# A weight chunk's low part by an accumulating transfer, in a two-layer decoder trunk

## The chip, the cores and the metric

The kernel runs on one core of a Trainium2 chip. The metric is the device time of one execution in microseconds (us); lower is better. Profiles show one execution, and their spans run from its first to its last instruction.

## What is computed

The trunk has two layers over 256 tokens of width 1024, batch 1, all in float32. Cut to what matters here:

```python
for l in range(DEPTH):                        # 2 layers
    h = rmsnorm(x, norm_g[l])
    q, k, v, ga, iq, ik, iw, xr, gr, ma, mb = split(h @ w_in[l])
    attn = dsa_attention(rope(q), rope(k), v, rope(iq), rope(ik), iw)   # top 64 keys by an indexer
    y_a = (attn * silu(ga)) @ w_out_attn[l]
    hr = rg_lru(conv4(xr), w_rg[l], w_ig[l], ...)                       # gates, then a scan over tokens
    y_b = (hr * silu(gr)) @ w_out_rnn[l]
    x = x + (sigmoid(ma) * y_a + sigmoid(mb) * y_b) @ w_o[l]
return rmsnorm(x, final_g)
```

## The kernel before

**Products in three passes.** A float32 product is made from float32r parts: a matrix W is split into a high part wh (W rounded to float32r) and a low part wl = W - wh, the activations likewise, and TensorE adds wh·h_high, wl·h_high and wh·h_low in PSUM (`mm3`, lines 640 to 644). So each 128x128 block of weights takes three matmuls.

**The weight stream.** The host lays all weights out as 225 chunks of 512 KB, 128 partitions by 1024 columns, 8 blocks each, in the order in which TensorE is to use them (`weight_stream`, and the class `Stream` from line 528). A chunk is loaded from SP's queue into one of four buffers `raw` (line 519). `chunk` (line 552) makes the two parts: `copy(wh, raw)`, a copy that rounds, and `sub(wl, raw, wh)`, a subtraction on VectorE (line 486 in the helper `tt`). The copy runs on ScalarE (line 480), or on VectorE (line 482) where the planner finds that ScalarE would begin it over 500 ns later. `wh` and `wl` have six buffers each (`WBUF`). The first two chunks are split in halves into other tiles (`whh`, `whl`).

**The order within a layer** (`plan`, line 65): the unit `head` (32 blocks: the index key, the index weights and three of the index queries) takes four chunks; then come the index queries `iq` 3, 4 and 5, a chunk each (in layer 0 these are chunks 4, 5 and 6), the first unit of `ga`, and after it the other index queries, the recurrent inputs `xr` and `gr`, the gates, the merge gates `ma` and `mb` and the rest of `ga`. All this is called the early part here: 492 blocks, 61.5 chunks, in each layer. Then follow `q`, `k`, `v` and the attention, and last the output projections `yb`, `ya` and `wo`. In `head`, the rotation (`rotate`, line 773) makes `ikr` from the bank `pk` with the tables `ctab_i` and `stab_i` (sines on ScalarE, lines 687 and 688) scaled to `ci` and `si`; `iwt` is the last reader of the bank `pk`, and `ga` needs a bank of that pool. From `ikr` come `kh` and `kl`, which the indexer's `dots` need (line 871); ScalarE takes their positive part as `rl`, and VectorE sums `rl` into `wk`. GpSimd masks `wk` with `affine_select` (`causal`, line 891, instruction on line 895), four times per layer.

**What sets the order.** No order is written by hand: `Program.issue` (line 285) is a list planner. Each operation has an engine, a planned cost and, after it, a planned latency by engine (`LATENCY`, line 227). Due times are carried back from TensorE's position in the stream (`deadlines`, line 371), weight conversions 2000 ns earlier (`LEAD`). `choose` (line 394) takes, for each engine, the candidate that can start first, then the one due first, and a buffer of a ring must be free in the plan. At the end the instructions are written out sorted by planned start (line 367), each engine's in that order; on the chip semaphores hold each one until what it needs is done. The planner's engines are TensorE, ScalarE, VectorE, GpSimd and SP's transfers.

The conversion, lines 566 to 571:

```python
                wh = pg.tile(wp, "wh", [P, 1024], F32R, nm("wh"), WBUF)
                wl = pg.tile(wp, "wl", [P, 1024], F32R, nm("wl"), WBUF)
                copy(wh, raw)
                sub(wl, raw, wh.bitcast(F32))
                pg.shift = 0.0
                self.parts[c] = (wh, wl)
```

Of the kernel before, what the change touches and what calls it, by code (L numbers as in the profile page):

```python
# [11 lines left out]
F32 = mybir.dt.float32  # L12
F32R = mybir.dt.float32r
I32 = mybir.dt.int32
AF = mybir.ActivationFunctionType
OP = mybir.AluOpType
# [4 lines left out]
L = 2  # L21
# [43 lines left out]
def plan(l):  # L65

    u = [("head",)]
    iq = [("iq", i) for i in range(8)]
    light = []
    for n, i in (("ga", 0), ("mb", 0), ("ga", 1), ("mb", 1), ("ga", 2), ("ma", 0), ("ga", 3), ("ma", 1)):  # L70
        light += [(n, 2 * i), (n, 2 * i + 1)] if n == "ga" else [(n, i, c) for c in range(4)]
    u += iq[3:NRAW]
    for i in range(NRAW, 8):
        u += light[:NMIX] + [iq[i]]
        light = light[NMIX:]
    for j in range(KR):
        u += [("xr", j), ("gr", j)]
        u += light[:2 if j % 3 == 0 else 1]
        light = light[2 if j % 3 == 0 else 1:]
        if j >= DELAY:  # L80
            u.append(("gate", j - DELAY))
    for j in range(KR - DELAY, KR):
        u += light[:2]
        light = light[2:]
        u.append(("gate", j))
    u += light
    for pr in range(4):
        u += [("q", 2 * pr), ("q", 2 * pr + 1), ("k", 2 * pr), ("k", 2 * pr + 1)]
        if pr % 2 == 0:
            u += [("v", pr // 2, c) for c in range(4)]  # L90
        u.append(("attn", pr))
    u += [("yb", n) for n in range(2)]
    if l == L - 1:
        return u + [("xt", 0), ("ya", 0), ("xt", 1), ("ya", 1), ("wt", 0), ("wt", 1)]
    u += [("ya", n) for n in range(2)]
    return (u + [("wo", m, 0, 4) for m in range(6)] + [("wo", m, 4, 8) for m in range(6)]
            + [("wo", m, 0, 8) for m in range(6, 8)])


def gate_parts(j):  # L100


    f = foreign(j)
    if 2 * len(f) <= P:
        return [("stack", f)]
    return [("plain", f[:-STACK]), ("stack", f[-STACK:])]
# [13 lines left out]
def unit_blocks(u):  # L120

    n = u[0]
    if n == "head":
        return [b for k in range(KD)
                for b in [("in80", k, OFF["ik"])] + [("in", k, OFF["iq"] + i * P) for i in range(3)]]
    if n in ("attn", "xt"):
        return []
    if n in ("iq", "ga", "xr", "gr", "q", "k"):
        return [("in", k, OFF[n] + u[1] * P) for k in range(KD)]
    if n == "gate":  # L130
        out = []
        for w in ("rg", "ig"):
            out.append((w, u[1], u[1] * P))
            out += [(w, tuple(rows * (2 if kind == "stack" else 1)), u[1] * P) for kind, rows in gate_parts(u[1])]
        return out
    if n in ("v", "mb", "ma"):
        return [("in", 2 * u[2] + k, OFF[n] + u[1] * 512 + a * P) for k in range(2) for a in range(4)]
    if n == "yb":
        return [("or", k, u[1] * 512 + a * P) for k in range(KR) for a in range(4)]
    if n == "ya":  # L140
        return [("oa", k, u[1] * 512 + a * P) for k in range(KD) for a in range(4)]
    if n == "wt":
        return [("o", k, u[1] * 512 + a * P) for k in range(KD) for a in range(4)]
    return [("o", k, u[1] * P) for k in range(u[2], u[3])]
# [3 lines left out]
NCH = -(-NBLK // 8)  # L148


class H:


# [55 lines left out]
def real(a):  # L209
    return a.ap() if isinstance(a, V) else a  # L210
# [12 lines left out]
TABS[AF.Sqrt] = ("sqrt",)  # L223
TABS[AF.Sin] = ("sin",)
PSUM_TAGS = ("pp", "pq", "pt")
ENGINES = ("pe", "act", "dve", "pool", "dma")
LATENCY = {"pe": 190.0, "act": 140.0, "dve": 130.0, "pool": 200.0, "dma": 2000.0}
TO_PE = 230.0
SWITCH = 1283.0

# [1 line left out]
class Program:  # L232
# [52 lines left out]
    def issue(self):  # L285
# [13 lines left out]
        for o in ops:  # L299
            for h in o.uses:  # L300
                left[id(h)] = h.users
        free = {e: 0.0 for e in ENGINES}
        pending = {e: [] for e in ENGINES}

# [13 lines left out]
        while n < total:  # L318
            best = None
            for e in ENGINES:  # L320
                c = self.choose(e, pending[e], free, slots, nalloc, given, table, pepos)
                if c is not None and (best is None or c[0] < best[0]):
                    best = c + (e,)
            if best is None:
                raise RuntimeError("no instruction can go: " + ", ".join(
                    f"{e}:{[(o.no, [h.name for h in o.new]) for o in pending[e][:4]]}" for e in ENGINES))
            s, o, e = best
# [22 lines left out]
            for h in o.uses:  # L350
                left[id(h)] -= 1
                if left[id(h)] == 0:
                    lst = slots[(h.pool, h.tag)]
                    lst.append(o.end + LATENCY[o.eng])
                    lst.sort()
            for q in o.succs:
                p = ops[q]
                lat = 0.0 if p.eng == o.eng == "pe" else LATENCY[o.eng] + (TO_PE if p.eng == "pe" else 0.0)
                p.ready = max(p.ready, o.end + lat)
# [11 lines left out]
    def deadlines(self):  # L371
# [8 lines left out]
        for o in reversed(ops):  # L380
# [5 lines left out]
            for h in o.uses:  # L386
                if id(h) in nxt and nxt[id(h)] > o.no:
                    t = min(t, d[nxt[id(h)]])
            d[o.no] = t - o.cost - LATENCY[o.eng]
        for o in ops:  # L390
# [42 lines left out]
def trunk(ctx, tc, xT, pos, pre, par, fgb, wst, out):  # L433
    nc = tc.nc
# [6 lines left out]
    pg = Program()  # L441
    cnt = [0]

    def nm(s):
        cnt[0] += 1
        return f"{s}{cnt[0]}"
# [5 lines left out]
    def r2(s):  # L452
        return pg.tile(rp, "r2", [P, 2, T], F32R, nm(s), R2)
# [22 lines left out]
    def copy(o, i):  # L476

        n = o.size()
        pg.op("act", (50 if i.psum() else 94) + 0.833 * n, [o], [i],
              lambda: nc.scalar.activation(real(o), real(i), AF.Copy),  # L480
              alt=(67 + 1.046 * n if i.psum() else 69 + 0.52 * n,
                   lambda: nc.vector.tensor_copy(real(o), real(i))))

    def tt(op, o, a, b):
        pg.op("dve", 67 + 1.046 * o.size(), [o], [a, b],
              lambda: nc.vector.tensor_tensor(real(o), real(a), real(b), op=op))  # L486
# [7 lines left out]
    def sub(o, a, b):  # L494
        tt(OP.subtract, o, a, b)
# [32 lines left out]
    class Stream:  # L528
# [23 lines left out]
        def chunk(self, c):  # L552
            if c not in self.parts:
                for _ in self.load(c + 1):
                    pass
                raw = self.raws.pop(c)
                pg.shift = -LEAD
                if c < HALVED:
                    self.parts[c] = []
                    for q in raw if c == 0 else (raw[:, :512], raw[:, 512:]):  # L560
                        t = r2("whh").join(), r2("whl").join()
                        split(t, q)
                        self.parts[c].append(t)
                    pg.shift = 0.0
                    return self.parts[c]
                wh = pg.tile(wp, "wh", [P, 1024], F32R, nm("wh"), WBUF)
                wl = pg.tile(wp, "wl", [P, 1024], F32R, nm("wl"), WBUF)
                copy(wh, raw)
                sub(wl, raw, wh.bitcast(F32))
                pg.shift = 0.0  # L570
                self.parts[c] = (wh, wl)
            return self.parts[c]
# [78 lines left out]
    def split(dst, src):  # L651

        copy(dst[0], src)
        sub(dst[1], src, dst[0].bitcast(F32))
# [8 lines left out]
    for bits in (6, 8, 8):  # L663
        q = 2.0 ** (math.floor(math.log2(rest)) - bits + 1)
# [655 lines left out]
```

## Time and profile before

| | us |
|---|---|
| median of 3 runs | 706.12 (705.9 to 706.37) |
| the profiled execution's own time | 705.1 |
| its span, first to last instruction | 703.3 |
| TensorE busy in it | 686.1 |

Rows of the profile name engines PE (TensorE's matmuls), PEld (its weight loads, beside PE), DVE (VectorE), ACT (ScalarE), POOL (GpSimd) and SP; a `q` behind a name is that engine's instruction queue. `wl<-raw,wh` is an instruction that writes tile wl and reads raw and wh, L486 the line of the kernel. A wait row says who waited for whom. Where an idle time stands in brackets, it is the engine's just before the instruction, and what ended it.

### The profile page before, as it was taken

What the parts mean: (1) busy time and instruction counts of PE and PEld (TensorE: products, weight loads), DVE (VectorE), ACT (ScalarE), POOL (GpSimd) and SP (SyncE); (2) the same over time, 40 slices, a digit from 0 to 9 for tenths busy, and PEclk for the clock granted to TensorE, in tenths of its full rate; (3) what the DMA queues carried; (4) which work ended last, traced back from release to release, by engine and by line L of the source; (5) the groups of instructions that cost most, each with busy time, mean ns of one, the idle gap of its engine ahead of it and who ended that gap; (6) DMA issues with size and microseconds to landing.
All of it is one profiled execution on the core that took longest, in us unless ns stands there. A gap on an engine that the chain in (4) does not pass through costs nothing.

```text
span 703.3 us, 12628 instructions
## 1 busy us (share of the span) xinstructions
PE 686.1 (98%) x4720; PEld 638.4 (91%) x4720; DVE 602.6 (86%) x1177; ACT 482.8 (69%) x775; POOL 6.4 (1%) x18
## 2 busy tenths in 40 slices
PE   7898999999999999999999999999999999999996
PEld 7898999999999998888999899999999898988885
DVE  7989999999897959857779997999989987796573
ACT  7996675799995748444558766588769765674433
POOL 0000000000000000000000000000000000000000
PEclk9999999999999999999999999999999999999999
DMA  8646566667756462655553655576666565535621
GB/s 292 195 157 211 159 197 201 203 189 220 223 177 189 149 192 75 205 180 179 173 173 111 213 178 163 177 220 207 210 205 185 182 190 163 180 101 171 195 73 60
DMA packets 38104, 125.24 MB, mean 178 GB/s; under 512 B 4892, under 2 KB 7260, under 8 KB 38044
## 3 DMA queue, kind: packets, MB, share of 16 engines
q1 hardware_dynamic: 38044, 124.44, 56.5%
q8 instruction: 37, 0.61, 0.3%
q14 instruction: 23, 0.19, 0.1%
HBM read 119.77 MB, written 1.05 MB: 172 GB/s over the span
## 4 chain that ended last, share of the span: by engine, by line
PE 82%; DVE 7%; ACT 6%; issue 2%; DMA 2%; SPq 0%; DVEq 0%; ACTq 0%
PE rps L512 14%; PE yb L512 9%; PE q L512 7%; PE k L512 7%; PE ops L512 6%; PE ma L512 6%; PE ya L512 6%; PE v L512 6%; PE gps L512 5%; PE ga L512 4%; PE mb L512 4%; DVE wl L486 2%; PE iq L512 2%; ACT wh L480 2%; PE lg L512 2%
## 5 line engine op out<-in xcount | busy, mean ns | idle before, releaser
L486 DVE TENSOR_TENSOR wl<-raw,wh 128x1024 fp32r<-128x1024 f32 x223 | 271.5, 1220 | 58.4 <-ACT wh L480 57.1
L480 ACT ACTIVATE wh<-raw 128x1024 fp32r<-128x1024 f32 x196 | 207.3, 1059 | 138.6 <-PE rps L512 21.4
L512 PE MATMUL rps<-hh,wh 128*128 128x256 f32 x352 | 99.5, 283 | 0.0
L512 PE MATMUL rps<-hl,wh 128*128 128x256 f32 x352 | 99.5, 283 | 0.0
L512 PE MATMUL rps<-hh,wl 128*128 128x256 f32 x352 | 99.5, 283 | 0.0
L512 PEld LDWEIGHTS rps<-hh,wl 128*128 128x128 f32 x352 | 67.4, 192 | 0.3
L512 PEld LDWEIGHTS rps<-hh,wh 128*128 128x128 f32 x352 | 67.3, 191 | 0.3
L512 PEld LDWEIGHTS rps<-hl,wh 128*128 128x128 f32 x352 | 67.4, 191 | 0.0
L512 PE MATMUL yb<-wh,g 128*128 128x512 f32 x176 | 59.0, 396 | 0.0
L512 PE MATMUL iq<-xg,wh 128*128 128x256 f32 x232 | 45.3, 285 | 0.0
L512 PE MATMUL ya<-wh,aT 128*128 128x512 f32 x128 | 40.8, 395 | 0.0
L512 PE MATMUL ga<-hh,wh 128*128 128x256 f32 x128 | 36.3, 283 | 2.0 <-DVE iwt L486 2.0
L512 PEld LDWEIGHTS iq<-xg,wh 128*128 128x128 f32 x232 | 37.4, 192 | 0.0
L512 PEld LDWEIGHTS yb<-wh,g 128*128 128x128 f32 x176 | 32.5, 188 | 5.3
L512 PE MATMUL q<-hh,wl 128*128 128x256 f32 x128 | 36.4, 284 | 0.0
L512 PE MATMUL q<-hh,wh 128*128 128x256 f32 x128 | 36.3, 284 | 0.0
L512 PE MATMUL ga<-hl,wh 128*128 128x256 f32 x128 | 36.3, 283 | 0.0
L512 PE MATMUL k<-hh,wl 128*128 128x256 f32 x128 | 36.3, 283 | 0.0
L512 PE MATMUL q<-hl,wh 128*128 128x256 f32 x128 | 36.2, 283 | 0.0
L512 PE MATMUL ga<-hh,wl 128*128 128x256 f32 x128 | 36.2, 283 | 0.0
L512 PE MATMUL k<-hh,wh 128*128 128x256 f32 x128 | 36.2, 283 | 0.0
L512 PE MATMUL k<-hl,wh 128*128 128x256 f32 x128 | 36.2, 283 | 0.0
(264 smaller groups left out, 1944.6 us busy)
## 6 DMA issues: line engine op xcount, KB each, us to landing
raw<-in_wst_dram SPq DMA_DIRECT2D x224, 512.0 KB, 4.0
xk<-xs SPq DMA_DIRECT2D x24, 48.0 KB, 3.5
out_dram<-z SPq DMA_DIRECT2D x4, 256.0 KB, 2.3
rah<-in_wst_dram SPq DMA_DIRECT2D x2, 256.0 KB
xr<-in_xT_dram SPq DMA_DIRECT2D x1, 512.0 KB
fg<-in_fgb_dram SPq DMA_DIRECT2D x2, 256.0 KB
xk<-xs SPq DMA_DIRECT2D x8, 40.0 KB
xf<-xs SPq DMA_DIRECT2D x2, 160.0 KB
```

Of the source, the lines that this page charges most:

```text
L480: lambda: nc.scalar.activation(real(o), real(i), AF.Copy),
L486: lambda: nc.vector.tensor_tensor(real(o), real(a), real(b), op=op))
L512: lambda: nc.tensor.matmul(real(o), real(w), real(m), start=start, stop=stop, skip_group_check=grp))
```

## The change

For chunks 6, 9, 12, ... 60 of layer 0 and 118, 121, ... 172 of layer 1, 19 in each, all in the early part, the subtraction is replaced. ScalarE writes wl = -raw, rounded to float32r, which is -wh. The copy wh follows as before. Then a transfer issued from GpSimd's queue reads the same chunk from memory again and adds it to wl in place, so that wl = W - wh. The planner gets a sixth engine, `sum`, with a cost of 2000 ns and a latency of 3500 ns for such a transfer. All other chunks stay as they are.

```diff
+def summed_chunks():
+    out, n = set(), 0
+    for l in range(L):
+        early = sum(len(unit_blocks(u)) for u in plan(l)[:plan(l).index(("q", 0))])
+        out.update(range(n // 8 + 6, (n + early) // 8, 3))
+        n += sum(len(unit_blocks(u)) for u in plan(l))
+    return out
+
+SUMMED = summed_chunks()
...
-ENGINES = ("pe", "act", "dve", "pool", "dma")
-LATENCY = {"pe": 190.0, "act": 140.0, "dve": 130.0, "pool": 200.0, "dma": 2000.0}
+ENGINES = ("pe", "act", "dve", "pool", "dma", "sum")
+LATENCY = {"pe": 190.0, "act": 140.0, "dve": 130.0, "pool": 200.0, "dma": 2000.0, "sum": 3500.0}
...
-                copy(wh, raw)
-                sub(wl, raw, wh.bitcast(F32))
+                if c in SUMMED:
+                    pg.op("act", 94 + 0.833 * 1024, [wl], [raw],
+                          lambda: nc.scalar.activation(real(wl), real(raw), AF.Copy, scale=-1.0))
+                    copy(wh, raw)
+                    pg.op("sum", 2000, [wl], [wl],
+                          lambda: nc.gpsimd.dma_start(real(wl), wst[c], accum_op=OP.add))
+                else:
+                    copy(wh, raw)
+                    sub(wl, raw, wh.bitcast(F32))
```

## Rows read from the trace of the kernel before

**Rows 1.** The page's head: span, and busy time, share and instructions by engine.

```profile
span 703.3 us, 12628 instructions
PE 686.1 (98%) x4720; PEld 638.4 (91%) x4720; DVE 602.6 (86%) x1177; ACT 482.8 (69%) x775; POOL 6.4 (1%) x18
```

**Rows 2.** TensorE's waits, whole span: us in total, times, longest us.

```profile
PE pk L512 <- ACT whh L480: 5.1, 1, 5.1
PE ga L512 <- DVE iwt L486: 2.0, 1, 2.0
PE dots L512 <- DVE kl L486: 1.5, 1, 1.5
PE dots L512 <- ACT rl L473: 1.5, 2, 1.1
PE mb L512 <- DVE ga L486: 0.7, 1, 0.7
```

**Rows 3.** Stretches: us, busy PE, PEld, DVE, ACT, POOL; PEclk, DMA share, GB/s.

```profile
17.00:46.00 29.00, 27.02 (x226) 26.84 (x225) 26.39 (x43) 27.39 (x41) 0.00 (x0) 1.00 0.62 200
46.00:62.00 16.00, 13.36 (x86) 11.62 (x85) 15.22 (x24) 12.69 (x20) 0.00 (x0) 1.00 0.45 152
366.00:403.00 37.00, 35.90 (x279) 34.74 (x278) 36.06 (x58) 31.42 (x48) 0.00 (x0) 1.00 0.48 153
...
40.00:195.00 155.00, 152.29 (x1111) 144.16 (x1110) 147.85 (x313) 124.25 (x200) 2.48 (x4) 1.00 0.63 192
```

**Rows 4.** The page's groups: busy us, mean ns of one, idle before.

```profile
L486 DVE TENSOR_TENSOR wl<-raw,wh 128x1024 fp32r<-128x1024 f32 x223 | 271.5, 1220 | 58.4 <-ACT wh L480 57.1
L480 ACT ACTIVATE wh<-raw 128x1024 fp32r<-128x1024 f32 x196 | 207.3, 1059 | 138.6 <-PE rps L512 21.4
```

**Rows 5.** Instructions on the tile raw: ns min/median/max; loads' time to landing.

```profile
L482 DVE CAST wh<-raw x27: 669/692/696, 93.3 to 671.7; 128x1024 fp32r<-128x1024 f32 x27
...
DMA to landing us min/median/max: 3.5/4.0/5.6
```

**Rows 6.** DMA: the queue's packets, MB and share of 16 engines; issues, median landing.

```profile
q1 hardware_dynamic: 38044, 124.44, 56.5%
...
raw<-in_wst_dram SPq DMA_DIRECT2D x224, 512.0 KB, 4.0
```

**Rows 7.** The chain that ended last, in order of time: start, us, what.

```profile
161.49 5.75 PE rps L512 x48
```

**Rows 8.** ScalarE's waits: us in total, times, longest us.

```profile
ACT wh L480 <- PE rps L512: 21.4, 18, 1.8
```

**Rows 9.** Timeline of layer 0's start, single instructions: start us, us, what.

```profile
17.71 1.07 ACT L480 ACTIVATE wh<-raw 128x1024 fp32r<-128x1024 f32 x1 [0.52 <-DMA raw<-in_wst_dram]
...
27.91 0.49 ACT L688 ACTIVATE ctab_i<-kk,hpi 128x256 f32<-128x256 f32 x1
...
28.44 0.43 DVE L486 TENSOR_TENSOR ci<-ctab_i,rstd 128x256 f32<-128x256 f32 x1 [0.74 <-ACT ctab_i L688]
...
30.29 0.41 DVE L486 TENSOR_TENSOR iwt<-pk,rstd 128x256 f32<-128x256 f32 x1
...
30.85 0.36 PE L512 MATMUL ga<-hh,wh 128*128 128x256 f32 x1 [1.98 <-DVE iwt L486]
```

**Rows 10.** Timeline of both layers' first dots: start us, us, what.

```profile
56.22 1.21 DVE L486 TENSOR_TENSOR wl<-raw,wh 128x1024 fp32r<-128x1024 f32 x1
57.46 0.42 DVE L486 TENSOR_TENSOR kl<-ikr,kh 64x256 fp32r<-64x256 f32 x1
...
57.93 0.39 PE L512 MATMUL dots<-kl,iqs 128*128 128x256 f32 x1 [1.55 <-DVE kl L486]
...
395.89 2.34 DVE L486 TENSOR_TENSOR wl<-raw,wh 128x1024 fp32r<-128x1024 f32 x2
...
402.50 0.39 PE L512 MATMUL dots<-kh,iqs 128*128 128x256 f32 x1 [1.10 <-ACT rl L473]
```

**Rows 11.** GpSimd's line 895: ns min/median/max, first and last start us.

```profile
L895 POOL TENSOR_SCALAR_AFFINE_SELECT wk<-wk x8: 300/456/1385, 98.1 to 461.8; 128x128 f32<-128x128 f32 x4, 128x256 f32<-128x256 f32 x4
```

## Prediction

> **What bounds the kernel now.** I read the page's head first. TensorE is busy 686.1 of 703.3 us, VectorE 602.6 and ScalarE 482.8 [rows 1]. A change that takes work off VectorE therefore cannot shorten the bulk; it can only close holes in TensorE's row, and 703.3 - 686.1 = 17.2 us is all that row has, its start and its tail included.
>
> So the next view is TensorE's own waits: 5.1 us for the first weights at the start, which this change does not touch, and 2.0 + 1.5 + 1.5 + 0.7 = 5.7 us later [rows 2]. Those 5.7 us are all that can be won. They end on VectorE tiles (iwt, kl, ga) or on rl of ScalarE. The table by stretch says why they sit early in each layer: in 46 to 62 us VectorE is busy 15.22 of 16 us, in 366 to 403 us 36.06 of 37, while in 17 to 46 us it is ScalarE that is fuller, 27.39 of 29 [rows 3]. TensorE's granted clock is 1.00 in all of these, so the clock plays no part.
>
> **What is removed and added.** There are 19 summed chunks per layer (6, 9, ... 60 and 118, 121, ... 172), 38 in all. Each loses a VectorE subtraction of 1.220 us [rows 4]: 38 x 1.22 = 46.4 us, of which 602.6 falls to about 556. Each gains a negation on ScalarE, one ACTIVATE of the same shape as the copy wh, 1.059 us [rows 4]: 40.2 us. Where ScalarE is late, the planner may hand the copy wh to VectorE, at 0.692 us [rows 5]; then VectorE gains only 1.22 - 0.69 = 0.53 us and ScalarE pays nothing. Outside the early holes both engines work beside TensorE, so these sums cost and win nothing there.
>
> Each also gains a transfer on GpSimd's queue that reads the chunk a second time: 38 x 0.524 = 19.9 MB more than the 124.44 MB of now [rows 6]. Nothing in the trace is such a transfer, so I bound it. Not below the quickest load of the same bytes, 3.5 us from issue to landing [rows 5]. For the upper end: it has to read the old wl as well as the chunk, so two loads one after the other, each as slow as the slowest seen: 2 x 5.6 = 11.2 us [rows 5]. I take one median load, 4.0 us [rows 6], plus one more pass of the bytes through the DMA engines. A pass is 56.5% of 703.3 us for 124.44 MB [rows 1, 6], 397 us, or 1.67 us for 0.524 MB; together 5.7 us. The planner in the diff allots 2.0 + 3.5 = 5.5 us, so its order is right for that value.
>
> **Whether TensorE must wait for it.** A chunk is 8 blocks of 3 matmuls; 48 matmuls take 5.75 us [rows 7], so a chunk lasts 2.88 us. There are six wl buffers: the one of chunk c comes free when TensorE is done with c - 6, and is wanted five chunks later, after 5 x 2.88 = 14.4 us. That conversions begin as soon as the buffer is free is seen in ScalarE's waits, where wh waits for TensorE's rps 18 times [rows 8]. After the negation, 14.4 - 1.06 = 13.3 us are left for the transfer: 5.7 us is hidden, and so is 11.2. The exception is chunk 6. Its raw data is there at 17.71 us, and it is used last before the 1.98 us hole that ends at 30.85 us [rows 9], so from about 30.85 - 1.98 - 2.88 = 25.99 us. The negation ends at 18.77, which leaves 7.2 us: 5.7 fits, 11.2 would hold TensorE 4.0 us.
>
> **The queues.** The transfer waits on GpSimd's queue for its negation. That queue holds little else: eight affine_selects, from 98.1 us on [rows 11], each of which needs VectorE's wk. A transfer put behind one is held until that wk is done. The program is written out in the order of planned starts, so this costs only what plan and chip disagree on, against 13.3 - 5.7 = 7.6 us of slack: nothing. SP's queue has the same loads in the same order. A summed chunk's raw buffer is released by ScalarE instead of VectorE, at or before the time of now: nothing or a small gain, and no TensorE wait hangs on it.
>
> **The holes, one by one.** (a) In the 1.55 us hole that ends at 57.93 us, a 1.21 us subtraction stands between the two kl on VectorE [rows 10]. Chunks 9, 12 and 15 have by then taken 3 x 1.22 us off its backlog, so I give back 1.1. (b) The other wait on rl there, 1.5 - 1.1 = 0.4, goes too [rows 2]. (c) In layer 1 two subtractions (2.34 us) stand at 395.89 us on VectorE ahead of kl, on which the dots of the 1.10 us hole hang [rows 10]; chunks 121, 124, 127 and 130 come at or before it, so the 1.1 us goes. (d) The 0.7 us before mb waits for ga, also queued on VectorE: I give 0.7. Together -3.3 us. (e) The 1.98 us hole follows a chain on ScalarE: ctab_i ends at 28.40, ci follows at 28.44, iwt starts at 30.29 [rows 9]. ScalarE is full there [rows 3], and chunk 6's negation is put ahead of this chain: +1.06, if the copy stays on ScalarE. Sum: -3.3 + 1.06 = -2.2 us.
>
> The profiled execution took 705.1 us of its own (span 703.3 and 1.8 around it), 1.0 under the median of 706.12. So 705.1 - 2.2 = 702.9, and on the median's footing **703.9 us**, 0.3% faster. About 0.2%, 1.4 us, is what a measurement of this kernel can tell from no change.
>
> **Rivals.**
>
> *Nothing measurable.* VectorE is relieved, but the planner gives the copies to it, the holes keep their length since they are ordered by dependences (sines, rotations, kl), and (e) eats the rest. With 0.53 instead of 1.22 us per chunk, -3.3 becomes -1.4, and with +1.06 the sum is -0.4: 705.7 us. For it: ScalarE is 94% full in 17 to 46 us [rows 3], just where copies would move. Against it: in layer 1 VectorE is the fuller one, 36.06 to 31.42 us [rows 3]. Chance 0.25.
>
> *Late at the start, slower.* The transfer takes 11.2 us, not 5.7. Chunk 6 then holds TensorE 4.0 us, with (e) +1.06 and -3.3 elsewhere: +1.8, 707.9 us; should chunk 9 be late as well, some 710. It decides from 7.2 us upwards. For it: the DMA engines are 62% busy in 17 to 46 us [rows 3], so the transfer shares them with loads. Against it: GpSimd's queue is empty there. Chance 0.13.
>
> *The DMA engines fill, slower.* In 40 to 195 us they are 0.63 busy [rows 3]. Some 17 summed chunks fall there. One pass each adds 17 x 1.67 / 155 = 0.18, two add 0.37: exactly 1.00. From there every tenth of a pass costs 17 x 0.167 = 2.8 us per layer; 2.3 passes cost 3 x 2.8 x 2 layers = 17 us, -2.2 besides: 721 us. For it: nothing bounds the passes but my reading. Against it: the share is of time that packets took, waits of their own included, so 1.00 need not be full. Chance 0.12. The Trainium skill ("DMA: Bandwidth & Descriptors", section "Issuing engines are not separate DMA queues") says that transfers issued by any engine run on the same 16 DMA engines and interleave; no run here shows it yet. By "Collectives: The Full Stack" (section "The bandwidth ceiling: the fold count and why AG ≠ RS ≠ AR") an add in a DMA costs a second source read and no more, which would be two passes, the very edge.
>
> *VectorE starves GpSimd, slower.* If GpSimd can prepare a transfer only between VectorE's instructions, it stretches as the affine_selects do: 456 ns at the median, 1385 at most [rows 11], a factor of 3. On 5.7 us that is 17 us, 3.8 more than the 13.3 there are, 38 times: +144 us; if the factor holds only for the part on GpSimd, about 1.4 us, it is +2.8 and hidden but for chunk 6. I price it between, at 712. Chance 0.05. The Trainium skill ("SBUF — State Buffer", section "SBUF: two separate sides") states this rule: while VectorE runs a copy in its two-port mode, GpSimd cannot write descriptors, and the transfer should be issued elsewhere. In this trace the candidates, such as the cast wh, last 0.69 us each [rows 5].
>
> **How the numbers follow.** The forecast (faster by over 0.2%) has 0.45, nothing measurable 0.25, the three slower cases 0.13 + 0.12 + 0.05 = 0.30. The low end is all of the 5.7 us gone: 706.1 - 5.7 = 700.4. The high end takes in the late start, chunk 9 included, and the stretched transfer, 714; left out is the case of full DMA engines and the tail of the last, some 0.15. The forecast's own range is 701 to 704.7.
>
> **What would show it.** Right: 185 subtractions instead of 223 on VectorE, VectorE near 556 us plus moved copies; 38 GpSimd transfers of 512 KB landing in under 7.2 us; TensorE's waits on kl, rl and ga near zero, and the one before 30.85 us about 1 us longer. Wrong: a TensorE wait on wl for a DMA, loads landing well above 4.0 us, a DMA share near 1 in 40 to 195 us, or holes of the old length at other places.

## The result and the profile after

The changed kernel takes 718.28 us (median; 717.62 to 720.35) against 706.25 for the kernel before, timed beside it: a ratio of 1.0175 with a 95% interval of 1.0153 to 1.0197, 12.0 us slower. The forecast was 703.9, the range ended at 714.0. The profiled execution took 717.62 us.

The page's head after the change answers to [rows 1].

```profile
span 715.8 us, 12713 instructions
PE 692.1 (97%) x4720; PEld 642.7 (90%) x4720; DVE 578.1 (81%) x1166; ACT 492.7 (69%) x786; POOL 45.6 (6%) x56
```

VectorE did become lighter, 602.6 to 578.1 us. But the span is 12.5 us longer, and TensorE is busy 6.0 us longer with the same 4720 matmuls. So there are two halves to explain: 6.5 us in which TensorE stands, and 6.0 us in which it does the same work more slowly.

TensorE's waits, as in [rows 2] (us in total, times, longest):

```profile
PE pk L526 <- ACT whh L494: 5.2, 1, 5.2
PE dots L526 <- ACT rl L487: 4.7, 1, 4.7
PE ga L526 <- DVE iwt L500: 3.4, 1, 3.4
PE mb L526 <- DVE iqr L500: 2.2, 2, 1.5
PE dots L526 <- ACT kh L494: 1.3, 1, 1.3
PE dots L526 <- DVE kl L500: 0.4, 1, 0.4
PE iq L526 <- DMA wl<-in_wst_dram: 0.2, 1, 0.2
```

Behind the start, which is as before, they add up to 12.2 us instead of 5.7: the first half. The wait on kl has nearly gone, as forecast; those on rl, iwt and iqr have grown. Hardly any of it, 0.2 us, is for the transfer itself.

The stretches of [rows 3], and three short ones of the same view (us, busy PE, PEld, DVE, ACT, POOL; PEclk, DMA share, GB/s):

```profile
17.00:46.00 29.00, 25.42 (x199) 25.04 (x198) 23.96 (x41) 23.67 (x34) 2.74 (x3) 0.94 0.80 232
46.00:62.00 16.00, 12.50 (x73) 10.69 (x72) 12.31 (x23) 14.67 (x21) 1.72 (x2) 0.94 0.68 187
366.00:403.00 37.00, 37.00 (x295) 36.21 (x295) 27.80 (x46) 30.89 (x46) 2.59 (x3) 1.00 0.74 196
40.00:195.00 155.00, 151.49 (x1109) 143.67 (x1108) 133.51 (x299) 125.68 (x202) 19.21 (x20) 0.99 0.90 247
...
32.60:36.00 3.40, 3.03 (x14) 3.06 (x15) 3.04 (x7) 3.35 (x6) 0.00 (x0) 0.50 0.78 254
59.90:63.30 3.40, 3.40 (x10) 2.67 (x9) 3.37 (x5) 3.25 (x4) 0.16 (x1) 0.50 0.77 119
411.50:418.30 6.80, 5.06 (x23) 5.06 (x24) 5.03 (x12) 2.90 (x6) 0.88 (x1) 0.50 0.94 299
```

The last three are the second half. In them the granted clock is 0.50, the lower of its two levels (1.2 instead of 2.4 GHz), for 3.4, 3.4 and 6.8 us: around the end of the hole before ga, behind a row of three short holes (1.5, 1.3 and 0.7 us, ending at 53.6, 57.9 and 58.9 us), and around the end of the hole in layer 1. TensorE is busy 3.03 + 3.40 + 5.06 = 11.5 us in them. If it does half as much there, 5.7 of the 6.0 us are explained, an estimate from these rows. Compare also 17 to 46 us with [rows 3]: ScalarE, with more to do, is busy *less*, 23.67 instead of 27.39 us. It waits.

What it waits for stands in the timeline. These lines answer to [rows 9], and the last four are layer 1's:

```profile
16.38 1.05 ACT L584 ACTIVATE wl<-raw 128x1024 fp32r<-128x1024 f32 x1
...
26.81 1.06 ACT L494 ACTIVATE wh<-raw 128x1024 fp32r<-128x1024 f32 x1 [2.21 <-DMA raw<-in_wst_dram]
...
30.42 0.49 ACT L709 ACTIVATE ctab_i<-kk,hpi 128x256 f32<-128x256 f32 x1
...
30.95 0.42 DVE L500 TENSOR_TENSOR ci<-ctab_i,rstd 128x256 f32<-128x256 f32 x1
...
32.41 0.41 DVE L500 TENSOR_TENSOR iwt<-pk,rstd 128x256 f32<-128x256 f32 x1
...
32.97 0.55 PE L526 MATMUL ga<-hh,wh 128*128 128x256 f32 x1 [3.39 <-DVE iwt L500]
...
392.55 1.06 ACT L494 ACTIVATE wh<-raw 128x1024 fp32r<-128x1024 f32 x1 [2.62 <-DMA raw<-in_wst_dram]
...
411.86 1.06 ACT L584 ACTIVATE wl<-raw 128x1024 fp32r<-128x1024 f32 x1 [0.25 <-DMA raw<-in_wst_dram]
412.82 0.85 ACT L487 ACTIVATE rl<-dots 128x256 f32<-128x256 f32 x2
...
413.24 0.58 PE L526 MATMUL dots<-kh,iqs 128*128 128x256 f32 x1 [4.69 <-ACT rl L487]
```

ScalarE works in order. In layer 0 it stands 2.21 us before a chunk that has not landed; the sines for ctab_i are queued behind that conversion, ci and iwt hang on them, and TensorE on iwt. In layer 1 the last step before the hole's end is a negation (line 584) that stands ahead of rl, on which dots hangs. The chain that ended last goes through these loads (start, us, what); the second stands before the row of short holes:

```profile
18.83 7.90 DMA raw<-in_wst_dram
...
39.04 7.92 DMA raw<-in_wst_dram
...
405.42 6.33 DMA raw<-in_wst_dram
```

7.90, 7.92 and 6.33 us from issue to landing, where the median before was 4.0 [rows 6] and the longest 5.6 [rows 5].

The loads are also in another order than before. A summed chunk is due earlier, since its transfer has to follow, and by the planner's order the changed kernel loads chunk 6 ahead of 5, 9 ahead of 8 and 127 ahead of 126. The first line above is chunk 6's negation, which starts before chunk 5 has been converted; the conversion at 26.81 us is chunk 8's, whose load stood behind that of chunk 9.

The groups and the DMA part of the page:

```profile
L500 DVE TENSOR_TENSOR wl<-raw,wh 128x1024 fp32r<-128x1024 f32 x185 | 225.6, 1221 | 68.1 <-ACT wh L494 66.4
L587 POOL DMA_DIRECT2D wl<-in_wst_dram x38 | 34.3, 903 | 474.6 <-ACT wl L584 234.2
L584 ACT ACTIVATE wl<-raw 128x1024 fp32r<-128x1024 f32 x38 | 40.2, 1057 | 19.4 <-PE rps L526 9.8
L496 DVE CAST wh<-raw 128x1024 fp32r<-128x1024 f32 x52 | 36.0, 692 | 15.3 <-PE rps L526 11.0
...
q1 hardware_dynamic: 38044, 124.44, 54.3%
q0 software_dynamic: 5472, 19.93, 15.7%
...
raw<-in_wst_dram SPq DMA_DIRECT2D x224, 512.0 KB, 4.7
wl<-in_wst_dram POOLq DMA_DIRECT2D x38, 512.0 KB, 8.4
```

The transfers land in 8.4 us at the median, and the loads beside them in 4.7. Queue q0 takes 15.7% of 715.8 us, 112.4 us or 2.96 us of all 16 engines per transfer, 1.8 of the 1.67 us passes. The planner gave 25 more copies to VectorE (52 instead of 27).

### The profile page after: what moved, and what is told of

Read it like the earlier page. It is cut to its first block, busy times and chain, and to the rows that moved or that the text cites. A ratio compares the mean times of both kernels' runs of the same rounds, so it can differ in the third digit from the quotient of the medians.

```text
span 715.8 us, 12713 instructions
## 1 busy us (share of the span) xinstructions
PE 692.1 (97%) x4720; PEld 642.7 (90%) x4720; DVE 578.1 (81%) x1166; ACT 492.7 (69%) x786; POOL 45.6 (6%) x56
## 3 DMA queue, kind: packets, MB, share of 16 engines
q0 software_dynamic: 5472, 19.93, 15.7%
## 4 chain that ended last, share of the span: by engine, by line
PE 88%; ACT 4%; DMA 4%; DVE 2%; issue 1%; SPq 0%; ACTq 0%; DVEq 0%
PE rps L526 16%; PE yb L526 8%; PE q L526 6%; PE k L526 6%; PE ops L526 6%; PE ma L526 6%; PE ya L526 6%; PE v L526 6%; PE ga L526 6%; PE mb L526 5%; PE gps L526 4%; PE iq L526 3%; DMA raw<-in_wst_dram 3%; PE dots L526 2%; PE lg L526 2%; PE av L526 2%
## 5 line engine op out<-in xcount | busy, mean ns | idle before, releaser
L500 DVE TENSOR_TENSOR wl<-raw,wh 128x1024 fp32r<-128x1024 f32 x185 | 225.6, 1221 | 68.1 <-ACT wh L494 66.4
L494 ACT ACTIVATE wh<-raw 128x1024 fp32r<-128x1024 f32 x171 | 180.8, 1058 | 124.2 <-PE ya L526 20.3
L587 POOL DMA_DIRECT2D wl<-in_wst_dram x38 | 34.3, 903 | 474.6 <-ACT wl L584 234.2
L584 ACT ACTIVATE wl<-raw 128x1024 fp32r<-128x1024 f32 x38 | 40.2, 1057 | 19.4 <-PE rps L526 9.8
L496 DVE CAST wh<-raw 128x1024 fp32r<-128x1024 f32 x52 | 36.0, 692 | 15.3 <-PE rps L526 11.0
L519 DVE SCALAR_TENSOR_TENSOR xc<-rps,prm,xc 128x255 f32<-128x255 f32 (+2 forms) x66 | 31.4, 475 | 6.1 <-ACT xc L487 5.8
```

The costliest lines, as they stand in the source:

```text
L519: lambda: nc.vector.scalar_tensor_tensor(real(o), real(a), real(s), real(b), op0=op0, op1=op1))
L584: lambda: nc.scalar.activation(real(wl), real(raw), AF.Copy, scale=-1.0))
L587: lambda: nc.gpsimd.dma_start(real(wl), wst[c], accum_op=OP.add))
```

## The experiments

Two theories were set against each other. A: the transfers slow SP's loads, and ScalarE, in order, stands before a late one with TensorE's feeders queued behind. B: the negations on ScalarE and the planner's new order make the holes, whatever the loads do. All times are medians beside the kernel before, which had 706.15 to 706.84 us.

**e1: an eighth of the bytes.**

```diff
-  nc.gpsimd.dma_start(real(wl), wst[c], accum_op=OP.add)
+  nc.gpsimd.dma_start(real(wl[:, :128]), wst[c][:, :128], accum_op=OP.add)
```

> The changed kernel, its order of instructions kept, but each of the 38 accumulating transfers moves 128 of the 1024 columns; seven eighths of those low parts are left as the negated high part. Theory A (the transfers slow SP's loads, ScalarE stands in order before a late raw, and what TensorE needs is queued behind it): raw's median landing back from 4.7 to 4.0 to 4.2 us, no ScalarE wait of over 1 us for raw after 15 us, time 703 to 708 us. Theory B (the negations on ScalarE and the new order themselves make TensorE's holes, whatever the loads do): still 715 to 719 us.

709.62 us, ratio 1.0053 (1.0035 to 1.0070): 3.5 us slower, between the two. With every instruction in the same order, the bytes alone make 12.0 - 3.5 = 8.5 us. The loads are back; the one that took 7.90 us takes 5.27. Head of the page, two of TensorE's waits, and the landings:

```profile
PE 689.7 (97%) x4720; PEld 641.4 (91%) x4720; DVE 578.2 (82%) x1166; ACT 492.8 (70%) x786; POOL 45.9 (6%) x56
...
PE dots L526 <- ACT rl L487: 2.6, 1, 2.6
PE ga L526 <- DVE iwt L500: 0.8, 1, 0.8
...
raw<-in_wst_dram SPq DMA_DIRECT2D x224, 512.0 KB, 3.9
wl<-in_wst_dram POOLq DMA_DIRECT2D x38, 64.0 KB, 5.1
```

Behind the start, TensorE's waits add up to 6.5 us, only 0.8 more than before. It is busy 3.6 us longer, and two stretches of 3.4 us show half clock. So most of what e1 still loses is lost to the clock.

**e2 and e3: where the summed chunks lie.** The range starts at the 18th chunk of a layer instead of the 6th (e2), or ends before the 18th (e3).

```diff
-  out.update(range(n // 8 + 6, (n + early) // 8, 3))
+  out.update(range(n // 8 + 18, (n + early) // 8, 3))   # e2
+  out.update(range(n // 8 + 6, n // 8 + 18, 3))         # e3
```

> Summed chunks from the 18th chunk of each layer on only (15 per layer instead of 19), so none in the first 60 us of a layer. Theory A, in its narrow form (only at a layer's start, where ScalarE and VectorE have no slack, does a late raw reach TensorE): 705.5 to 707.5 us, although raw's median landing stays near 4.6 us. Theory B, if each negation costs its share: 15/19 of 12 us, 715 us. If the DMA engines being 0.9 busy is the cost, as in the rival of the prediction: 713 to 716 us.

> Only the first four summed chunks of each layer (6, 9, 12, 15 and 118, 121, 124, 127), eight in all. Theory A, narrow form: all of the loss or nearly, 715 to 719 us, with ScalarE waits on raw of about 2 us in layer 0. If the loss is spread over the 38 transfers: 8/38 of 12 us, 708 to 709 us.

e3 717.55 us, ratio 1.0159 (1.0142 to 1.0176): eight summed chunks make 11.4 of the 12 us. e2 714.18, ratio 1.0115 (1.0094 to 1.0135), against the narrow form of A and inside the range of busy DMA engines; e5 decides between these. Its trace offers a reason: conversions run ahead, so chunk 130 still fell before layer 1's hole, which was 3.33 us long, and ScalarE waited 3.0 us for raw just before it ended. The cut was set too early.

```profile
ACT wl L584 <- DMA raw<-in_wst_dram: 3.4, 2, 3.0
```

**e5: the cut set later**, `n // 8 + 30`.

> Summed chunks from the 30th chunk of each layer on only, 11 per layer; their conversions fall after both layers' first dots. In e2 chunk 130 was still converted at about 395 us, before the hole at 405. Theory A, narrow form (a late load reaches TensorE only where ScalarE and VectorE have no lead, at a layer's start): 705.3 to 707.3 us, no hole and no half clock beyond those of before, although raw lands in 4.5 us or more at the median beside the transfers and the DMA share in 110 to 185 us stays over 0.85. If the load of the DMA engines costs wherever it falls: 22/38 of 12 us, 712 to 714 us.

706.04 us, ratio 0.9995 (0.9986 to 1.0004): 22 summed chunks cost nothing and bring nothing. The stretch, and the landings:

```profile
110.00:185.00 75.00, 75.00 (x565) 72.10 (x564) 65.79 (x149) 60.33 (x101) 10.68 (x11) 1.00 0.96 271
...
raw<-in_wst_dram SPq DMA_DIRECT2D x224, 512.0 KB, 4.4
wl<-in_wst_dram POOLq DMA_DIRECT2D x22, 512.0 KB, 8.2
```

The DMA engines are 0.96 busy and TensorE works 75.00 of 75 us. So a share near 1 is no bound by itself; the place is what matters.

One part of the expectation failed. The profile has a longer hole at layer 0's start than before, and 3.4 us of half clock behind it:

```profile
PE ga L526 <- DVE iwt L500: 3.4, 1, 3.4
...
ACT wh L494 <- DMA raw<-in_wst_dram: 4.4, 6, 2.0
```

The first transfer of e5 is issued at 96.64 us. Still, a load issued at 15.04 us took 6.27 us to land, ScalarE stood 2.0 us before it, and the hole that ended at 32.10 us was 3.44 us long, like that of the changed kernel. So a load can be late at a layer's start with no transfer before it. What ties the loss to the transfers is not this hole in one profile but the medians of e1 and e3, and layer 1.

**e4: the same bytes, overwriting.** The transfer without `accum_op`.

> The changed kernel, its order kept, but the 38 transfers overwrite wl with the chunk instead of adding to it, so the low parts are wrong and the bytes read from memory the same. If it is the reading of the destination that makes the transfer long and the loads late: this one lands in 4 to 6 us instead of 8.4, raw near 4.3, time 704 to 710 us. If it is the second reading of the chunk from memory alone: landing 7 to 8.4 us, raw 4.7, time 715 to 719 us.

711.27 us, ratio 1.0068 (1.0052 to 1.0085): 5.1 us slower instead of 12.0, just above the range for the first reading. The transfer's queue and its landing:

```profile
q0 software_dynamic: 5472, 19.93, 9.1%
...
wl<-in_wst_dram POOLq DMA_DIRECT2D x38, 512.0 KB, 6.1
```

9.1% of its 710.0 us span is 1.70 us of 16 engines each, one pass; the accumulating one took 2.96. Adding costs 1.7 times the DMA time of overwriting, and 7 us of the kernel.

**e6 and e12: the planner told.** Both latencies as the chip shows them (e6), or the transfer's alone (e12).

```diff
-  "dma": 2000.0, "sum": 3500.0
+  "dma": 4500.0, "sum": 6400.0   # e6
+  "dma": 2000.0, "sum": 6400.0   # e12
```

> The changed kernel with the planner told what the chip shows: a load lands 2.5 us later than planned before (latency 4500 instead of 2000), a transfer in 8.4 us (latency 6400 instead of 3500). Theory A: what hurts is that ScalarE's order was planned for loads that land in 3.6 us; told, it puts other work ahead of the conversions, ScalarE's waits for raw fall from 5.4 us to under 2, time 706 to 713 us. If the order has no part in it and the loads alone starve the start: 716 us or more.

> The changed kernel with only the transfer's planned latency mended (6400 instead of 3500), the loads' left at 2000. If it is the loads, planned to land in 3.6 us, that ScalarE stands before: 713 to 719 us, with ScalarE's waits on raw of 4 us or more as in the changed kernel. If the planned time of the transfer made the bad order: 706 to 710 us, as e6.

e6 707.92 us, ratio 1.0028 (1.0017 to 1.0040); e12 716.28, ratio 1.0140 (1.0119 to 1.0161). The transfer's time alone wins back 2 us, both times 10: the loads' planned time is what counts. With it mended, ScalarE's waits for raw fall from 7.7 us (5.4 for wh and 2.3 for the negations) to

```profile
ACT wl L584 <- DMA raw<-in_wst_dram: 0.2, 1, 0.2
```

and 10 of the 12 us are gone, with the same transfers, the same bytes and about the same work on ScalarE (494.6 us busy, 492.7 in the changed kernel). The order is another one, of loads too: chunks 6 and 9 are back in their places. In e12 they are not, and ScalarE still waits 7.9 us.

**e8 and e9: the negation on VectorE**, with full transfers (e8) and with those of 128 columns (e9).

```diff
-  pg.op("act", 94 + 0.833 * 1024, [wl], [raw],
-        lambda: nc.scalar.activation(real(wl), real(raw), AF.Copy, scale=-1.0))
+  tsc(wl, raw, -1.0, None, OP.mult)
```

> The changed kernel with the negation on VectorE (a multiplication by -1, about the 0.69 us of its cast) and the full transfers kept, so ScalarE has no more work than before. Theory A (late loads before an in-order ScalarE): still 714 to 719 us, ScalarE waiting for raw by 2 us at a time. If the negation on ScalarE carries the loss: 705 to 709 us.

> The fourth corner beside the change, e1 and e8: negation on VectorE and transfers of 128 columns (seven eighths of the low parts left as the negated high part). Full transfers cost 8.6 us with the negation on ScalarE (e1 against the change). Theory A+B (late loads and the negations hurt through the same place, ScalarE's full queue, so that each costs little without the other): 704.5 to 706.5 us, and late loads then cost only 2 to 4 us with the negation on VectorE (e8 against this). Theory A alone (late loads cost 8 us whatever ScalarE does): would need 700 us here. Theory B alone: 708 to 709, as e8.

e8 708.65 us, ratio 1.0035 (1.0023 to 1.0047): theory A alone falls. ScalarE waits longer for loads than in the changed kernel, yet the loss is 2.4 us:

```profile
ACT wh L494 <- DMA raw<-in_wst_dram: 9.4, 6, 3.3
```

e9 703.77 us, ratio 0.9966 (0.9955 to 0.9977): faster than the kernel before by 2.5 us, below the range of A+B (704.5 to 706.5) and above the 700 of A alone. The four corners, in us against the kernel before:

| | 512 KB each | 64 KB each |
|---|---|---|
| negation on ScalarE | +12.0 | +3.5 |
| negation on VectorE | +2.4 | -2.5 |

The bytes cost 8.5 or 4.9 us, the negation's place 9.6 or 6.0, and 3.6 us come only when both meet. Along a row of the table the order of instructions is the same; down a column it is not, since the planner wrote it anew, so the negation's share holds that of the new order. Both rows load chunks 6, 9 and 127 early, so that alone does not cost: e9 is the fastest of all. So both theories hold and share a place, ScalarE's queue at a layer's start. The corner -2.5 is what a partly relieved VectorE is worth, beside transfers that carry little.

**e7: VectorE relieved by GpSimd**, which subtracts for the 38 chunks.

> The relief of VectorE alone: the same 38 chunks get their subtraction on GpSimd instead, with no negation, no transfer and no second reading. If relieving VectorE by 38 subtractions at these places is worth what the prediction said, 3.3 us, and GpSimd's 2.4 us (planned, not measured) do not slow VectorE: 702.5 to 704 us. If the holes hang on the order of ScalarE and not on VectorE's load: 705.5 to 707.5. If GpSimd and VectorE hold each other up: over 708, with subtractions on VectorE longer than 1.22 us.

721.50 us, ratio 1.0216 (1.0199 to 1.0233), the slowest of all. Its subtraction and VectorE's cast:

```profile
L585 POOL TENSOR_TENSOR wl<-raw,wh 128x1024 fp32r<-128x1024 f32 x38 | 100.4, 2642 | 419.4 <-ACT wh L494 373.0 <-DVE wh L496 40.0 <-DVE sd L522 6.5
...
L496 DVE CAST wh<-raw 128x1024 fp32r<-128x1024 f32 x25 | 21.1, 845 | 2.8 <-PE iq L526 1.4 <-PE ya L526 0.7 <-PE rps L526 0.7
```

GpSimd needs 2.64 us, more than planned. VectorE is slower beside it, as in the third reading: its casts go from 692 to 845 ns at the mean, its scans from 679 to 946, its subtractions from 1220 to 1250. Whether the slower VectorE or the later wl made the holes was not separated, so e7 does not say what relief alone is worth.

**e10: both remedies.**

> Both remedies: negation on VectorE and the planner told the landing times of the chip. If the two mend separate losses: 704 to 706 us. If both mend the one place, ScalarE's queue at a layer's start: no better than the better of e6 and e8, 706.5 to 709 us.

711.11 us, ratio 1.0076 (1.0059 to 1.0094): worse than either alone, and expected by neither. The planner writes a new order for each set of costs, and this one is poor; which step of it is at fault stays open.

**e13 and e14: a hole alone.** In the kernel before, TensorE is made to wait ahead of layer 0's first q for 24 (e13) or 10 (e14) ScalarE copies of 128 columns.

```diff
+            if self.l == 0 and hd == 0:
+                z, s = const("zz", [P]), self.sma[1, 1]
+                pg.op("act", 10, [z], [s], lambda: [nc.scalar.activation(real(z), real(s[:, :P]), AF.Copy)
+                                                    for _ in range(24)][-1])
+                trans(bank("pt", "zps")[:, 0, :P], z)
```

> The kernel before, without any summed chunk or transfer, with one hole made on purpose: ahead of layer 0's first q, near 195 us, TensorE waits for 24 small ScalarE copies, some 5 us, that the planner counts as nothing. If a hole alone brings the half clock behind it: 3.4 to 6.8 us of granted clock 0.5 right after the hole, and the time rises by the hole and 1.7 to 3.4 us more: 711 to 716 us. If the half clock comes with the transfers or a layer's start: no half clock there, and the time rises by the hole alone, 710 to 712 us.

> The same with 10 copies, a hole of some 2 us, about that which the kernel before has at 28.9 us without a half clock behind it in its profile, and e2, e5 and e10 with one. If the hole alone decides: 708 to 709 us without a half clock, or 709.5 to 711 us with one of 3.4 us.

e13 716.71 us, ratio 1.0143 (1.0126 to 1.0160), just above its range; e14 710.72, ratio 1.0053 (1.0035 to 1.0070); beside 706.84. In e13's profile the hole is 7.65 us long and ends at 204.15 us. The clock falls at 200.07, with no transfer in the program. The first three stretches are e13's, the last is e14's, behind its hole of 2.88 us:

```profile
195.00:204.20 9.20, 1.55 (x14) 1.35 (x13) 2.46 (x4) 8.47 (x28) 0.00 (x0) 0.78 0.29 101
204.20:206.90 2.70, 2.70 (x13) 2.70 (x14) 2.07 (x4) 2.68 (x4) 0.00 (x0) 0.50 0.00 0
206.90:210.00 3.10, 3.10 (x28) 3.10 (x27) 1.69 (x6) 2.53 (x6) 0.00 (x0) 1.00 0.53 153
...
199.80:203.20 3.40, 3.40 (x29) 3.40 (x30) 2.75 (x7) 3.37 (x6) 0.00 (x0) 1.00 0.01 5
```

In e13 TensorE is busy all of 204.2 to 206.9 and issues 13 matmuls there, in the 3.1 us after it 28. e14's profile shows full clock behind its hole; its half clock lies at 31.4 us, behind the kernel's own hole of 1.75 us. So a hole can bring the half clock by itself. Its length alone does not decide: a hole of 3.07 us was followed by half clock (e10, at 29.6 us), one of 3.04 us was not (e12, at 411.6 us).

**e11: a version ahead of both.** Negation on VectorE as in e8, and summed chunks in layer 1 only.

```diff
+  out.update(range(n // 8 + 6, (n + early) // 8, 3) if l else ())
```

> Summed chunks in layer 1 alone (19), with the negation on VectorE. In e8 layer 1 came out 1.1 us ahead of the kernel before (its 1.1 us hole at 401 us was gone) and layer 0 lost 3.3. Theory A+B: 704.7 to 705.9 us, a gain of 0.3 to 1.5 us from that hole. If e8's layer 1 was luck of one execution: 706 to 708 us.

705.12 us, ratio 0.9986 (0.9977 to 0.9995): 1.2 us ahead of the kernel before, less than the 1.4 us that the prediction took as the least one can tell, though the interval leaves out 1. TensorE's waits on rl are 0.6 us instead of 1.5 [rows 2], since the 1.1 us hole of layer 1 is 0.2 us long:

```profile
PE dots L526 <- ACT rl L487: 0.6, 2, 0.4
```

## Why the prediction was wrong

**What bounds, and where the gain lies: right; its size is not shown.** The 5.7 us of waits early in each layer were the prize, and a relieved VectorE closes part of them: -2.5 us in e9, where they add up to 4.4 us. That this is near the sum of -2.2 is luck. e9 has no negation on ScalarE, so -3.3 stands against it, and VectorE keeps a negation of 0.69 us per chunk, by which the prediction's own scaling gives -1.4. Nor did the holes go as listed: (c) is gone in e9 and 0.2 us long in e11, (d) is 0.2 us, but what the wait on kl in (a) lost, 1.0 us, came back on rl, 1.7 us. In the changed kernel itself the wait on kl shrank from 1.5 to 0.4 us.

**The transfer's time: too small, within its bounds.** 8.4 us at the median (5.4 to 10.3) where 5.7 was taken between 3.5 and 11.2. The estimate counted the second pass about rightly (1.8 passes measured, 2 assumed) but added it to the 4.0 us of a load from SP's queue; from GpSimd's queue an overwriting transfer already takes 6.1 us (e4). That TensorE would hardly wait for it was right: 0.2 us, at chunk 6, whose transfer took 8.8 us. The 7.2 us of slack were mis-sized, since chunk 6 was loaded early: its negation began at 16.38 us, not 17.71.

**The step that failed: the queues.** It put SP's loads at "nothing or a small gain, and no TensorE wait hangs on it", because the queue has the same loads in the same order. The order is not the same: the planner put chunks 6, 9 and 127 ahead of their neighbours. And the same loads take longer: they share the DMA engines with the transfers, land in up to 9.1 us instead of 5.6, and at a layer's start ScalarE stands before them in order. Seven eighths of the bytes taken away, 8.5 of 12 us are gone (e1); told of the landing times, the planner wins back 10 (e6). The contention was seen, but only as a delay of the transfer and as a bound on throughput in 40 to 195 us, where it costs nothing (e5, in 110 to 185 us); it should have been priced as latency of the loads, at the place with no lead. The Trainium skill's rule quoted there ("DMA: Bandwidth & Descriptors", section "Issuing engines are not separate DMA queues") agrees with the trace: raw's median went from 4.0 to 4.7 us. The other one, by which an add costs a second source read, stands in the Trainium skill for the reduce step of a collective ("Collectives: The Full Stack", section "The bandwidth ceiling: the fold count and why AG ≠ RS ≠ AR"); here the DMA time is 2.96 us against 1.70 without the add, 1.7 times and not quite twice.

**Term (e): mis-sized, and at the wrong hole.** One negation was charged, +1.06 us before ga in layer 0. With the loads nearly in time (e1) that hole is 0.8 us instead of 2.0, while the one on rl in layer 1 is 2.6 instead of 1.1 and half clock follows. Negations at the first chunks of both layers stand in the queue that feeds the rotations and rl; taking them off ScalarE, with the order that the planner then writes, is worth 6.0 us with little traffic and 9.6 with much.

**Left out: the clock.** "The clock plays no part" held for the kernel before. The longer holes and the row of short ones brought 13.6 us of half clock, 5.7 to 6.0 of the 12.5 us of span; no term or rival had it.

**The rivals.** "Late at the start" had the place right and the mechanism wrong: it is the loads that are late, not the transfer. "The DMA engines fill" is refuted by e5, 0.96 busy at no loss. "VectorE starves GpSimd" does not show at its size: the transfers' instructions on GpSimd last 903 ns at the mean and 1.38 us at most beside a VectorE busy 81% of the span, and no transfer of the changed kernel took over 10.3 us, where that rival had 17. The Trainium skill's rule ("SBUF — State Buffer", section "SBUF: two separate sides") is not tested by this: how much of a landing VectorE's copies cost, no run here shows.

## What to carry to other kernels

A second stream of DMA is to be priced as latency for the loads that are there already, at the stage where their consumer has no lead; a busy share near 1 where conversions run chunks ahead cost nothing here. Where instructions are put in order by a planner, its costs have to hold under the new load as well, or an in-order engine stands before the late tile with everything else behind it. And a hole in TensorE can cost more than its length: the one of 7.65 us in e13 cost 9.9 us, with half clock in its last 4.1 us and for 2.7 us behind it.

## What was not expected of the hardware

An accumulating transfer of 64 KB still takes 5.1 us to land, and one of 512 KB 8.4, so more than half of it does not go with the bytes (the queue's packets are 5472 in both); an overwriting one of 512 KB from the same queue takes 6.1. Holes of 1.75 to 2 us before ga were followed by 3.4 us of half clock in some profiles (e2, e14) and by full clock in others (1.98 us in the kernel before, 1.82 in e13), which single profiles of a kernel with such holes do not settle.
